# A two-layer diffusion trunk on one core: the row sum of the Fourier output weights made by an adding DMA, and an activation table loaded earlier

## The chip, the cores and the metric

The kernel runs on one core of a Trainium2 chip. The metric is device time in microseconds (us), from runs of the whole program; lower is better. Engines carry the profile's names: PE (TensorE matmul; PEld is its weight load), DVE (VectorE), ACT (ScalarE), POOL (GpSimd) and SP (SyncE, which here only issues DMAs). "Row" in the profile means one line of one of its views.

## The reference, cut to what matters

Everything is float32, with 512 latent tokens, 1024 channels, 256 context tokens and two layers. Layer 0 is attention, layer 1 is Fourier mixing with a linear map behind it; each ends with a gated convolutional feed-forward net. `rms_norm` stands before and behind every sub-layer, and each norm needs one reciprocal square root per token.

```python
def rms_norm(x, g):
    xf = x.astype(F32)
    y = xf * lax.rsqrt(jnp.mean(xf * xf, axis=-1, keepdims=True) + EPS)
    return (y * g.astype(F32)).astype(x.dtype)

def fourier_mix(h):
    b, l, d = h.shape
    hg = h.reshape(b, l, FNET_GROUPS, d // FNET_GROUPS).astype(F32)
    f = jnp.fft.fft2(hg, axes=(1, 3), norm="ortho").real
    return f.reshape(b, l, d).astype(h.dtype)

def conv_ffn(h, w_up, conv_w, conv_b, w_down):
    u = h @ w_up
    up = jnp.pad(u, ((0, 0), (1, 1), (0, 0)))
    u = up[:, :-2] * conv_w[0] + up[:, 1:-1] * conv_w[1] + up[:, 2:] * conv_w[2] + conv_b
    gate, val = jnp.split(u, 2, axis=-1)
    return (jax.nn.silu(gate) * val) @ w_down

# layer i:
h = modulate(rms_norm(x, norm_g[i, 0]), sh1, sc1)
y = attention_mixers(...) if i % 2 == 0 else fourier_mix(h) @ w_f
x = x + g1 * rms_norm(y, norm_g[i, 1])
h = modulate(rms_norm(x, norm_g[i, 2]), sh2, sc2)
x = x + g2 * rms_norm(conv_ffn(h, ...), norm_g[i, 3])
```

In the cosine and sine sums of the Fourier transform, channel c of a group of 256 and channel 256 - c share their values up to a sign. So `fourier_mix(h) @ w_f` needs, per group, only 128 rows of cosine sums times the sum of two rows of `w_f`, and 128 rows of sine sums times their difference. Making these sums and differences is what the main part of the change touches.

## The kernel before, in words

**Product.** A float32 product is made of three matmuls in a reduced-precision type. `split` rounds a tile to a high part (an ACT copy, `wh`, line 125) and takes the rest as a low part (a DVE subtraction, `wl`, the same line). `mm3` (lines 102 to 104) then issues high times high, high times low and low times high. In the profile, L102, L103 and L104 are these three. A weight tile can be used by L102 and L103 as soon as `wh` stands, and by L104 only when `wl` stands too.

**Order.** The program is written in one order, with priorities, and a scheduler places each engine's instructions in a queue of that engine's own; every queue runs in order. `fence` and `held` keep some instructions behind an earlier point of their engine. Tiles come from pools with a fixed number of places: `raw` (weights as loaded, by SP) has three, `wh` and `wl` have five each.

**Norms.** A column sum of squares is made by small matmuls (L184) into a `misc` tile. `rstd` (lines 187 to 195) makes the reciprocal root: an ACT table function gives `st_r` (L190), DVE scales the mean to `st_v` (L191), and a Newton step follows on DVE (L192 to L194). `spread` (L215) lays the result on a diagonal, a matmul (L218) carries it to all partitions, and ACT copies it out (L219). `rstd_all` (lines 201 to 210) does the same at the program's end on a wide tile. The ACT function needs a table of its own, and the feed-forward net's gate function (L1268) needs another; where the next function's table isn't there, the row `ACT_TABLE_LOAD` stands ahead of it.

**Feed-forward.** `ffn` has groups of up-projection, convolution, gate and down-projection. The last down phase of a layer (where `end` is true, line 1417) has no gate left in it. It runs over eight channel blocks d for the first half of the tokens, and then again for the second half; `mid`, between the two, starts the norm of the first half.

**Fourier output.** `w_f` is stored in eight tiles d, one per block of 128 output channels, each 128 partitions by 4 groups by 2 rows by 128 channels, 512 KB. Two tiles are loaded early into free places of `yT` (`fourier_load`, L1551); the other six go through `raw`. `fourier_weights(d)` makes the sum of the two rows (L1559: on DVE for d = 0, on POOL for the others) and their difference (L1560, DVE) in a third tile, and splits that. Each d then takes twelve matmuls with the difference (operand `B` in the profile), three with the Nyquist row (`N`) and twelve with the sum (`A`); DVE puts the two together (L1619, L1623).

**Beside it.** During this stage `up_weights_dma` fetches the first four up-projection weights of the layer behind it without using DVE. POOL issues a plain load into `xh` (L1118, 512 KB each). ACT writes the negative of its rounded value into `xl`, and POOL issues a second DMA of the same weights that adds into `xl` (L1122, the last one L1128). A DMA that adds is thus already in use four times. Its queue, the software queue of POOL, is apart from the hardware queue of SP. POOL also adds up squares (L277).

Of the kernel before, what the change touches and what calls it, by code (L numbers as in the profile page):

```python
# [10 lines left out]
F32 = mybir.dt.float32  # L11
# [68 lines left out]
def kernel(ctx: ExitStack, tc: tile.TileContext, a):  # L80
# [106 lines left out]
    def rstd(ps):  # L187
        w = ps.shape[1]
        v, t, r = (mk(cp, [P, W4], F32, "st_" + c, 2)[:, :w] for c in "vtr")
        S.activation(out=r, in_=ps, func=AF.Abs_reciprocal_sqrt, bias=eps, scale=1.0 / D)  # L190
        V.tensor_scalar(out=v, in0=ps, scalar1=1.0 / D, scalar2=EPS, op0=ALU.mult, op1=ALU.add)  # L191
        V.tensor_tensor(out=t, in0=r, in1=r, op=ALU.mult)  # L192
        V.scalar_tensor_tensor(out=t, in0=t, scalar=-0.5, in1=v, op0=ALU.mult, op1=ALU.mult)
        V.scalar_tensor_tensor(out=v, in0=t, scalar=1.5, in1=r, op0=ALU.add, op1=ALU.mult)  # L194
        return v
# [5 lines left out]
    def rstd_all(ps):  # L201
        ps = ps[:, :HT]
        r, t, v = (mk(cp, [P, HT], F32, "md_t", 4) for _ in range(3))
        R = mk(cp, [P, HT], F32, "Rs", 3)
        S.activation(out=r, in_=ps, func=AF.Abs_reciprocal_sqrt, bias=eps, scale=1.0 / D)
        S.activation(out=v, in_=ps, func=AF.Identity, bias=eps, scale=1.0 / D)
# [1025 lines left out]
    def ffn(l, xp, ready, pre, mid, gem, plain=None):  # L1232
# [146 lines left out]
        for gi, (f0, nch) in enumerate(GROUPS[l]):  # L1379
# [37 lines left out]
            if end:  # L1417
                pump(gem, 100)
                fence()
# [29 lines left out]
    with ExitStack() as es:  # L1449
# [98 lines left out]

        def fourier_load(d):
            r = yT[:, 3 * d + 1:3 * d + 3, :].rearrange("p a (g i c) -> p (a g) i c", i=2, c=P)  # L1550
# [3 lines left out]
        def fourier_weights(d, eng=G):  # L1554
            r = f_first[d] if d < 2 else raw([P, 4, 2, P], a["w_f"][d])

            pm = (yT[:, 6:8, :] if d in (3, 5) else yT[:, 2:4, :] if d == 1 else mk(cp, [P, 2, T], F32, "gacc")).rearrange(
                "p a (g c) -> p a g c", g=4)
            held(eng.tensor_tensor(out=pm[:, 0, :, :], in0=r[:, :, 0, :], in1=r[:, :, 1, :], op=ALU.add))  # L1559
            held(V.tensor_tensor(out=pm[:, 1, :, :], in0=r[:, :, 1, :], in1=r[:, :, 0, :], op=ALU.subtract))  # L1560
            wh, wl = wpair([P, 2, 4, P])
            split(wh, wl, pm)
# [24 lines left out]
        f_first = [fourier_load(d) for d in range(2)]  # L1587
# [7 lines left out]
        w_f = [fourier_weights(0, V)]  # L1595
# [8 lines left out]
        for d in range(KC):  # L1604
            wh, wl = w_f.pop() if w_f else fourier_weights(d)
            if d in (1, 3, 4, 5, 6):
# [78 lines left out]
def _layout(i):  # L1685
# [36 lines left out]
    w_f = np.stack([lo, hi], 1).reshape(4, 2, P, KC, P).transpose(3, 2, 0, 1, 4)  # L1722
# [22 lines left out]
```

## Time and profile before

| what | value |
|---|---|
| median of 3 runs (lowest to highest) | 1143.04 us (1142.85 to 1143.35) |
| the profiled execution: time, span | 1143.02 us, 1141.3 us |
| mean granted TensorE clock | 0.996 |
| busy PE, DVE, ACT, POOL in the span | 1113.0, 899.9, 595.6, 177.9 us |
| Fourier output stage: first and last matmul begin | 717.18, about 750.6 us |
| table load before `st_r` at the end of layer 0, of layer 1 | 664.51, 1112.78 us, 1.28 us each |

Times in the trace are counted from the start of the span. A timeline row gives start, duration, engine, line, operation, output and inputs; the bracket at its end is the engine's idle time before it, and which instruction ended it. A windows row gives, for one stretch, the length and then busy time and count for PE, PEld, DVE, ACT and POOL, the granted clock as a share of full speed, the share of the 16 DMA engines that was busy, and the GB/s.

### The profile page before, as it was taken

How to read it: one execution, taken by the hardware profiler on the slowest of the kernel's cores; microseconds unless marked ns; L12 is line 12 of the kernel's file. 1: busy time of each engine (PE TensorE's matmuls, PEld its weight loads, DVE VectorE, ACT ScalarE, POOL GpSimd, SP SyncE). 2: the span in 40 equal slices, each digit the busy share in tenths (PEclk: the TensorE clock that was granted, in tenths of full speed). 3: DMA queues.
4: the chain of work that ended last, by engine and by line, in shares of the span. 5: the costliest groups of instructions: out<-in, count | busy, mean ns of one | idle time of the engine just before them, and what ended most of it. 6: DMA issues, size and time to landing. Idle time of an engine off the chain costs nothing.

```text
span 1141.3 us, 19565 instructions
## 1 busy us (share of the span) xinstructions
PE 1113.0 (98%) x7810; PEld 965.9 (85%) x7810; DVE 899.9 (79%) x1469; ACT 595.6 (52%) x1068; POOL 177.9 (16%) x180
## 2 busy tenths in 40 slices
PE   9999999999999999999999999999999999999995
PEld 5689888868898978887898898779888898899995
DVE  4678777765679976987999668978998998879755
ACT  4342355665665633552465446557746555555533
POOL 1236422421420000000000143620000000000012
PEclk9999999999999999999999999999999999999998
DMA  9675101075143355535534401742215533323332
GB/s 367 258 240 212 38 1 38 27 264 190 38 186 111 109 196 213 222 120 203 195 108 174 131 5 59 233 119 109 74 47 165 185 103 116 103 91 94 103 143 74
DMA packets 33763, 155.83 MB, mean 137 GB/s; under 512 B 3460, under 2 KB 8196, under 8 KB 22024
## 3 DMA queue, kind: packets, MB, share of 16 engines
q1 hardware_dynamic: 32520, 150.39, 37.0%
q0 software_dynamic: 1152, 4.19, 1.6%
q8 instruction: 61, 1.00, 0.3%
q14 instruction: 30, 0.25, 0.1%
HBM read 148.28 MB, written 6.29 MB: 135 GB/s over the span
## 4 chain that ended last, share of the span: by engine, by line
PE 83%; DVE 10%; ACT 3%; issue 2%; DMA 1%; POOL 1%; DVEq 0%; POOLq 0%; ACTq 0%; SPq 0%
PE mm L102 24%; PE mm L103 22%; PE mm L104 22%; DVE wl L125 2%; PE PT L950 1%; DVE md_t L302 1%; PE O L102 1%; PE gm L527 1%; DMA raw<-in_w_up 1%; PE O L103 1%; PE gm L102 1%; PE gm L104 1%; PE gm L103 1%; PE O L104 1%; PE mm L178 1%
## 5 line engine op out<-in xcount | busy, mean ns | idle before, releaser
L125 ACT CAST wh<-raw 128x1024 fp32r<-128x1024 f32 (+2 forms) x207 | 190.6, 933 | 169.8 <-PE mm L103 118.7
L125 DVE TENSOR_TENSOR wl<-raw,wh 128x1024 fp32r<-128x1024 f32 (+2 forms) x197 | 214.8, 1098 | 54.3 <-ACT wh L125 54.0
L102 PE MATMUL mm<-hh,wh 128*128 128x256 f32 (+1 forms) x632 | 206.4, 327 | 1.5 <-ACT yT L925 0.9
L104 PE MATMUL mm<-hh,wl 128*128 128x256 f32 (+1 forms) x632 | 203.7, 323 | 0.0
L103 PE MATMUL mm<-hl,wh 128*128 128x256 f32 (+1 forms) x632 | 203.5, 322 | 0.0
L277 POOL TENSOR_TENSOR gacc<-gacc,sq 128x256 f32<-128x256 f32 (+1 forms) x33 | 27.9, 847 | 717.0 <-ACT sq L275 716.2
L102 PEld LDWEIGHTS mm<-hh,wh 128*128 128x128 f32 x632 | 118.9, 188 | 17.7 <-ACT sq L1194 4.4
L103 PEld LDWEIGHTS mm<-hl,wh 128*128 128x128 f32 x632 | 118.9, 188 | 11.1
L104 PEld LDWEIGHTS mm<-hh,wl 128*128 128x128 f32 x632 | 118.9, 188 | 10.5 <-DVE wl L125 0.4
L102 PE MATMUL mm<-zh,wh 128*128 128x256 f32 x384 | 109.1, 284 | 1.4 <-ACT sq L1197 0.8
L102 PE MATMUL mm<-xh,wh 128*128 128x512 f32 (+1 forms) x302 | 107.5, 356 | 0.0
L103 PE MATMUL mm<-xl,wh 128*128 128x512 f32 (+1 forms) x302 | 106.8, 354 | 0.0
L103 PE MATMUL mm<-zl,wh 128*128 128x256 f32 x384 | 106.6, 278 | 0.0
L104 PE MATMUL mm<-zh,wl 128*128 128x256 f32 x384 | 106.4, 277 | 0.0
L104 PE MATMUL mm<-xh,wl 128*128 128x512 f32 (+1 forms) x302 | 106.2, 352 | 0.0
L102 PEld LDWEIGHTS mm<-zh,wh 128*128 128x128 f32 x384 | 72.3, 188 | 5.7 <-ACT sq L1197 4.4
L103 PEld LDWEIGHTS mm<-zl,wh 128*128 128x128 f32 x384 | 72.2, 188 | 0.0
L104 PEld LDWEIGHTS mm<-zh,wl 128*128 128x128 f32 x384 | 72.1, 188 | 0.0
L102 PEld LDWEIGHTS mm<-xh,wh 128*128 128x128 f32 x302 | 56.8, 188 | 9.9 <-issue 1.6
L103 PEld LDWEIGHTS mm<-xl,wh 128*128 128x128 f32 x302 | 56.8, 188 | 8.6 <-issue 0.4
L104 PEld LDWEIGHTS mm<-xh,wl 128*128 128x128 f32 x302 | 56.7, 188 | 8.6
L1255 ACT ACTIVATE cv<-mm,cols 128x512 f32<-128x512 f32 x59 | 45.9, 777 | 28.6 <-PE mm L104 22.2
(435 smaller groups left out, 2802.3 us busy)
## 6 DMA issues: line engine op xcount, KB each, us to landing
raw<-in_w_up SPq DMA_DIRECT2D x42, 1024.0 KB, 4.9
xT<-in_mod_r SPq DMA_DIRECT2D x20, 1024.0 KB, 5.2
raw<-in_w_down SPq DMA_DIRECT2D x32, 384.0 KB, 3.1
raw<-in_mod_p SPq DMA_DIRECT2D x8, 1024.0 KB, 4.9
raw<-in_w_down SPq DMA_DIRECT2D x16, 512.0 KB, 4.1
raw<-in_w_in SPq DMA_DIRECT2D x6, 1024.0 KB, 7.8
yT<-in_mod_r SPq DMA_DIRECT2D x10, 512.0 KB, 6.5
raw<-in_w_out SPq DMA_DIRECT2D x4, 1024.0 KB, 5.0
```

The costliest lines, as they stand in the source:

```text
L102: i = PE.matmul(out, lhsT=ah, rhs=bh, start=start, stop=False, skip_group_check=skip)
L103: PE.matmul(out, lhsT=ah, rhs=bl, start=False, stop=False, skip_group_check=skip)
L104: return i, PE.matmul(out, lhsT=al, rhs=bh, start=False, stop=stop, skip_group_check=skip)
L125: i = S.copy(out=h, in_=src), eng.tensor_tensor(out=l, in0=src, in1=f(h), op=ALU.subtract)
L178: PE.matmul(ps[:32, :src.shape[1]], lhsT=ones32, rhs=src, start=True, stop=True)
L277: G.tensor_tensor(out=self.acc[:, sl], in0=self.acc[:, sl], in1=sq[:, sl], op=ALU.add)
L302: m = V.scalar_tensor_tensor(out=t, in0=yT[:, k, hs], scalar=der[:, l, gi, k:k + 1], in1=R, op0=ALU.mult, op1=ALU.mult)
L527: PE.matmul(ps[32 * q:32 * q + 32, :], lhsT=spad[:, k, :], rhs=w[:, q * T:(q + 1) * T], start=k == 0, stop=k == KC - 1)
L950: PE.transpose(out=pt[:, j * P:(j + 1) * P], in_=Ps[j][:, off:off + P], identity=ident)
L1255: S.activation(out=cv, in_=ps, func=AF.Identity, bias=bc, scale=wc[1])
```

## The change

It has four parts.

1. **rstd**: the DVE scaling of the mean stands ahead of the ACT function instead of behind it. Both read the same PSUM tile.
2. **rstd_all**: the same, and the scaling moves from ACT (an `Identity`, L206) to DVE.
3. **Table**: at the start of each layer's last down phase, ACT runs the reciprocal-root function once on a column of the last gated tile, with scale 0, into a scratch column. Its table is thus loaded there.
4. **Fourier weights**: `w_f` is stored with the two rows outermost (2 by 4 groups by 128). Three tiles instead of two are loaded early into `yT`. `fourier_pair(d)` makes the difference in place, over the second row (DVE), and then lets a DMA issued by POOL add the second row, read again from HBM (256 KB), to the first row in place. Pairs are written three tiles ahead of the weights that use them, and `split` takes the tile as it then stands. The POOL and DVE additions and the third tile are gone.

```diff
     def rstd(ps):
...
+        V.tensor_scalar(out=v, in0=ps, scalar1=1.0 / D, scalar2=EPS, op0=ALU.mult, op1=ALU.add)
         S.activation(out=r, in_=ps, func=AF.Abs_reciprocal_sqrt, bias=eps, scale=1.0 / D)
-        V.tensor_scalar(out=v, in0=ps, scalar1=1.0 / D, scalar2=EPS, op0=ALU.mult, op1=ALU.add)
...
     def rstd_all(ps):
...
+        V.tensor_scalar(out=v, in0=ps, scalar1=1.0 / D, scalar2=EPS, op0=ALU.mult, op1=ALU.add)
         S.activation(out=r, in_=ps, func=AF.Abs_reciprocal_sqrt, bias=eps, scale=1.0 / D)
-        S.activation(out=v, in_=ps, func=AF.Identity, bias=eps, scale=1.0 / D)
...
             if end:
+                S.activation(out=once, in_=g_[-1][0][:, 0:1].bitcast(F32), func=AF.Abs_reciprocal_sqrt, bias=eps, scale=0.0)
                 pump(gem, 100)
                 fence()
...
         def fourier_load(d):
-            r = yT[:, 3 * d + 1:3 * d + 3, :].rearrange("p a (g i c) -> p (a g) i c", i=2, c=P)
+            r = yT[:, 2 * d + 1:2 * d + 3, :].rearrange("p i (g c) -> p i g c", c=P)
             SY.dma_start(out=r, in_=a["w_f"][d])
             return r
-        def fourier_weights(d, eng=G):
-            r = f_first[d] if d < 2 else raw([P, 4, 2, P], a["w_f"][d])
-            pm = (yT[:, 6:8, :] if d in (3, 5) else yT[:, 2:4, :] if d == 1 else mk(cp, [P, 2, T], F32, "gacc")).rearrange(
-                "p a (g c) -> p a g c", g=4)
-            held(eng.tensor_tensor(out=pm[:, 0, :, :], in0=r[:, :, 0, :], in1=r[:, :, 1, :], op=ALU.add))
-            held(V.tensor_tensor(out=pm[:, 1, :, :], in0=r[:, :, 1, :], in1=r[:, :, 0, :], op=ALU.subtract))
+        pairs_f = {}
+        def fourier_pair(d):
+            r = pairs_f[d] = f_first[d] if d < 3 else raw([P, 2, 4, P], a["w_f"][d])
+            held(V.tensor_tensor(out=r[:, 1], in0=r[:, 1], in1=r[:, 0], op=ALU.subtract))
+            G.dma_start(out=r[:, 0], in_=a["w_f"][d][:, 1], accum_op=ALU.add)
+        def fourier_weights(d):
             wh, wl = wpair([P, 2, 4, P])
-            split(wh, wl, pm)
+            split(wh, wl, pairs_f[d])
             return wh, wl
...
-        f_first = [fourier_load(d) for d in range(2)]
+        f_first = [fourier_load(d) for d in range(3)]
...
-        w_f = [fourier_weights(0, V)]
+        fourier_pair(0)
+        fourier_pair(1)
+        w_f = [fourier_weights(0)]
+        fourier_pair(2)
...
             wh, wl = w_f.pop() if w_f else fourier_weights(d)
+            if d + 3 < KC:
+                fourier_pair(d + 3)
...
-    w_f = np.stack([lo, hi], 1).reshape(4, 2, P, KC, P).transpose(3, 2, 0, 1, 4)
+    w_f = np.stack([lo, hi], 1).reshape(4, 2, P, KC, P).transpose(3, 2, 1, 0, 4)
```

The change also moves instructions in the queues, since the scheduler places them anew. Three places matter.

POOL in the Fourier output stage, before. `gacc`, `yT` and `raw` hold weights of `w_f`; `xh` and `xl` are the up-projection weights; `acc` adds up squares. The words in brackets are what an instruction waits for (DMAHW and DMASW: a hardware or software DMA).

```order
L1559 TENSOR_TENSOR yT_68<-yT_68 128x512 [waits DMAHW5_49,DMAHW4_49,DVE_49]
L1559 TENSOR_TENSOR yT_68<-raw_7845 128x512 [waits DMAHW6_49]
L1118 DMA xh_7750<-in_w_up 128x1024 [waits PE_49,Activation_49]
L1118 DMA xh_7752<-in_w_up 128x1024 [waits PE_49]
L1118 DMA xh_7754<-in_w_up 128x1024
L1118 DMA xh_7756<-in_w_up 128x1024
L1559 TENSOR_TENSOR gacc_7801<-raw_7799 128x512 [waits DMAHW3_49,DVE_49]
L1559 TENSOR_TENSOR gacc_7893<-raw_7891 128x512 [waits DMAHW7_49,DVE_49]
L1122 DMA xl_7751<-in_w_up 128x1024 [waits Activation_49]
```

Two of the seven additions stand ahead of the `xh` loads here. POOL now, at the same place:

```order
L1562 DMA raw_7713<-in_w_f 128x512 [waits DMAHW3_49,DMAHW2_49,DVE_49]
L1118 DMA xh_7761<-in_w_up 128x1024 [waits PE_49,Activation_49]
L1562 DMA raw_7757<-in_w_f 128x512 [waits DMAHW7_49,DVE_49]
L1118 DMA xh_7763<-in_w_up 128x1024 [waits PE_49]
L1118 DMA xh_7765<-in_w_up 128x1024
L1118 DMA xh_7767<-in_w_up 128x1024 [waits DMASW0_49]
L1562 DMA raw_7814<-in_w_f 128x512 [waits DMASW1_49,DMAHW0_49,DVE_49,Activation_49]
L1122 DMA xl_7762<-in_w_up 128x1024 [waits DMASW2_49,Activation_49]
L1122 DMA xl_7764<-in_w_up 128x1024 [waits DMASW3_49,PE_49,Activation_49]
L277 TENSOR_TENSOR acc_7751<-acc_7751,sq_7807 128x512 [waits Activation_49]
L1562 DMA raw_7859<-in_w_f 128x512 [waits DMAHW1_49,DMASW4_49,DVE_49]
L1122 DMA xl_7766<-in_w_up 128x1024 [waits DMASW5_49,Activation_49]
```

The seven additions are gone from POOL. Ahead of these rows stand three adding DMAs (d = 0 to 2); those of d = 3 and 4 stand before and among the `xh` loads, that of d = 5 before the adding `xl` loads, that of d = 6 behind two of them, and that of d = 7 behind three.

DVE in the middle of the same stage, now. `wl_7811`, `wl_7856` and `wl_7902` are the low parts for d = 2, 3 and 4; L1628 and L1632 are the lines that were L1619 and L1623.

```order
L125 TENSOR_TENSOR wl_7811<-yT_68,wh_7810 128x1024 [waits DMASW2_49,Activation_49]
L1628 TENSOR_TENSOR yT_68<-mm_7730,qs_7746 128x256 [waits PE_49,Activation_49]
L1561 TENSOR_TENSOR raw_7814<-raw_7814 128x512 [waits DMAHW0_49]
L125 TENSOR_TENSOR wl_7856<-raw_7713,wh_7855 128x1024 [waits DMASW3_49]
L1632 TENSOR_TENSOR yT_68<-mm_7730,qs_7746 128x255 [waits Activation_49]
L125 TENSOR_TENSOR wl_7902<-raw_7757,wh_7901 128x1024 [waits DMASW5_49,DVE_49]
```

Every low part now waits for its adding DMA (DMASW), and behind it on DVE stands the work of an earlier d.

DVE at the norm of the first half at the end of layer 0, before:

```order
L191 TENSOR_SCALAR st_v_6973<-misc_6964 128x64 [waits Activation_49]
L192 TENSOR_TENSOR st_t_6974<-st_r_6975 128x64
L1281 TENSOR_TENSOR yT_68<-yT_68,mm_7046 128x256 [waits PE_49]
L193 SCALAR_TENSOR_TENSOR st_t_6974<-st_t_6974,st_v_6973 128x64 [waits DVE_49]
L194 SCALAR_TENSOR_TENSOR st_v_6973<-st_t_6974,st_r_6975 128x64 [waits DVE_49]
L215 TENSOR_TENSOR Rs_6981<-st_v_6973,con_66 128x256 [waits DVE_49]
```

Here an instruction that waits for PE stands inside the norm's chain. DVE now, at the same place:

```order
L190 TENSOR_SCALAR st_v_6974<-misc_6965 128x64 [waits PE_49]
L192 TENSOR_TENSOR st_t_6975<-st_r_6976 128x64 [waits Activation_49]
L193 SCALAR_TENSOR_TENSOR st_t_6975<-st_t_6975,st_v_6974 128x64 [waits DVE_49]
L194 SCALAR_TENSOR_TENSOR st_v_6974<-st_t_6975,st_r_6976 128x64 [waits DVE_49]
L215 TENSOR_TENSOR Rs_6982<-st_v_6974,con_66 128x256 [waits DVE_49]
L1281 TENSOR_TENSOR yT_68<-yT_68,mm_7047 128x256 [waits PE_49]
```

The scaling waits for PE instead of ACT (and ACT's function, now L191, waits for DVE), and the chain is no longer broken by L1281, which waits for a later matmul. On PE, L218 of this norm now stands behind 16 matmuls after the column sum instead of 29. On ACT, the table load has left its place just ahead of `st_r` and stands as L1419 behind the last gated tile, eighteen instructions ahead of `st_r`.

## The prediction

> **What bounds the kernel now.** I read the page's first lines and the chain of waits, then a table by stretch of the Fourier output stage, then the timelines of that stage and of the two norms that the change touches.
>
> ```profile
> span 1141.3 us, 19565 instructions
> PE 1113.0 (98%) x7810; PEld 965.9 (85%) x7810; DVE 899.9 (79%) x1469; ACT 595.6 (52%) x1068; POOL 177.9 (16%) x180
> PE 83%; DVE 10%; ACT 3%; issue 2%; DMA 1%; POOL 1%; DVEq 0%; POOLq 0%; ACTq 0%; SPq 0%
> ```
>
> PE is busy for 98% and holds 83% of the chain. A cut on DVE or POOL is worth something only where PE waits or its matmuls are spread. The stage that the main edit touches is such a place:
>
> ```profile
> 716.00:720.00 4.00, 3.19 (x22) 2.52 (x20) 4.00 (x7) 2.54 (x6) 4.00 (x4) 1.00 0.00 0
> 720.00:729.00 9.00, 8.58 (x58) 7.42 (x59) 6.93 (x13) 4.48 (x9) 4.50 (x5) 1.00 0.98 330
> 729.00:732.00 3.00, 3.00 (x28) 3.00 (x26) 3.00 (x2) 0.95 (x3) 3.00 (x4) 1.00 0.38 93
> 732.00:751.00 19.00, 17.64 (x138) 15.70 (x140) 14.77 (x19) 12.02 (x22) 12.51 (x10) 1.00 1.02 274
> 717.18 0.28 PE L102 MATMUL mm<-B,wh 128*128 128x256 f32 x1
> 744.98 0.38 PE L102 MATMUL mm<-N,wh 4*128 4x258 f32 x1
> 748.62 0.38 PE L102 MATMUL mm<-N,wh 4*128 4x258 f32 x1
> 750.36 0.29 PE L102 MATMUL mm<-A,wh 128*128 128x258 f32 x1
> 735.47 0.39 PE L104 MATMUL mm<-B,wl 128*128 128x256 f32 x1 [0.76 <-DVE wl L125]
> PE mm L104 <- DVE wl L125: 2.3, 4, 0.8
> ```
>
> From one Nyquist matmul to the next is one tile d: 748.62 - 744.98 = 3.64 us when nothing is late. Eight tiles want 29.1 us. The last tile's final group begins at 750.36, so after three matmuls 0.12 us apart the stage is through at about 750.75, 33.6 after 717.18. So 4.5 us are lost, 2.3 of them as waits for the DVE low part. And the DMA engines, idle from 716 to 720, are full (0.98, 1.02) for 28 of the next 31 us.
>
> **The change: removed work.** The third tile's arithmetic is what makes DVE late.
>
> ```profile
> 714.23 0.68 DVE L1560 TENSOR_TENSOR gacc<-yT 128x512 f32<-128x512 f32 x1
> 735.67 3.09 DVE L1560 TENSOR_TENSOR gacc<-raw 128x512 f32<-128x512 f32 x1
> 740.15 1.21 DVE L125 TENSOR_TENSOR wl<-gacc,wh 128x1024 fp32r<-128x1024 f32 x1
> 715.09 1.05 ACT L125 CAST wh<-gacc 128x1024 fp32r<-128x1024 f32 x1
> 735.50 1.47 POOL L1559 TENSOR_TENSOR gacc<-raw 128x512 f32<-128x512 f32 x1
> ```
>
> A difference takes 0.68 us alone and up to 3.09 while POOL adds beside it. Per tile DVE then needs 0.68 + 1.21 and two combinations, well under 3.64. If the sums are in time, DVE is out of the way and the eight tiles take 29.1 us.
>
> **What it adds in front.** The first tile used to be summed by DVE in 0.68 us. Now its sum is a DMA. The nearest rows are those that POOL already issues: first `xh` (512 KB, plain), then `xl` (512 KB, adding); the last two rows are the software queue over 716 to 729 us (only `xh`: packets, MB, share of 16 engines) and over 729.4 to 755 (only `xl`).
>
> ```profile
> 718.90 2.35 POOL L1118 DMA_DIRECT2D xh<-in_w_up  x4
> DMA to landing us min/median/max: 4.3/5.8/7.6
> 737.99 1.06 POOL L1122 DMA_DIRECT2D xl<-in_w_up  x1
> DMA to landing us min/median/max: 5.4/8.8/12.0
> q0 software_dynamic: 576, 2.10, 50.9%
> q0 software_dynamic: 576, 2.10, 43.7%
> ```
>
> The four plain transfers held 0.509 x 13 = 6.6 us of all engines, 1.65 each; the four adding ones 0.437 x 25.6 = 11.2, 2.8 each. A 256 KB sum is bounded by half of a plain one (0.8) and a whole adding one (2.8); I take half of an adding one, 1.4, the same kind by its bytes. The fastest plain landing, 4.3, less its 1.65 leaves 2.65 us of fixed latency; so a lone sum lands 2.65 + 1.4 = 4.0 us after its issue. The difference for d = 0 ends at about 714.4 (it takes the place of L1559), the sum lands at 718.5, ACT rounds it by 719.6 (1.05), DVE has the low part by 720.9 (1.21). PE's new order uses the high part in seven matmuls (0.9 us) before it needs the low one, so it starts at 719.7 instead of 717.18 and waits 0.3 more: 2.8 us later than now. Without another delay the stage is through at 719.7 + 0.3 + 29.1 = 749.1 instead of 750.75: **-1.7 us**. POOL itself gains time: an adding issue holds it for about 1.06 us, an addition for 1.47 at 735.50.
>
> [...]
>
> **What it adds behind.** The sums of d = 0 to 3 fall mostly into the idle 716 to 720. The later ones meet full engines. From 720 on, ahead of and with the sum of d = 6: four `xh` 6.6, about 1.6 left from the first four sums (5.6 less 4.0), sums of d = 4 and 5 2.8, `raw` of d = 6 1.6 (as a plain 512 KB), two `xl` 5.6, itself 1.4: 19.6 us, so 739.6, and landed a good us later, or earlier by what SP's queue leaves behind it. Then 1.05 + 1.21 + hand-overs = 2.35: low part at 742 to 743. PE wants it at 719.7 + 0.3 + 6 x 3.64 + 0.4 = 742.2. For d = 7 come one more `xl` 2.8, `raw` of d = 7 1.6 and itself 1.4, and part of a 1 MB `raw` load that is queued by SP: landing 743.5 to 747, low part 746 to 749.5; wanted at 745.9. So the stage's end is late by 0 to 4 us; I take 2.5. **Fourier stage: -1.7 + 2.5 = +0.8 us** (bounds: -1.7 if no sum is late; with 2.8 a sum, 1.4 x 8 = 11 more engine time, of which the idle stretches hide about 3: +9).
>
> Who waits behind a late sum: on DVE the combinations of d = 4, and so the PSUM places of d = 7, which needs the same sum anyway; on SP the 1 MB `raw` loads, whose casts come only at 765; the last `xl`, issued behind the sum of d = 7 and used from 757.4, landed in all likelihood by 755.
>
> ```profile
> 757.41 0.50 PE L102 MATMUL mm<-hh,xh 128*128 128x258 f32 x2
> 765.20 1.98 ACT L125 CAST wh<-raw 128x1024 fp32r<-128x1024 f32 x2
> ```
>
> **Table and scaling.** The norm at the end of layer 0, from its column sum on, and an ACT row from the start of the same down phase:
>
> ```profile
> 664.71 0.32 PE L184 MATMUL misc<-sq,ones 128*32 128x64 f32 x8
> 664.51 1.28 ACT L190 ACT_TABLE_LOAD   x1
> 665.80 0.32 ACT L190 ACTIVATE st_r<-misc,eps 128x64 f32<-128x64 f32 x1
> 666.29 0.22 DVE L192 TENSOR_TENSOR st_t<-st_r 128x64 f32<-128x64 f32 x1
> 667.54 0.22 DVE L193 SCALAR_TENSOR_TENSOR st_t<-st_t,st_v 128x64 f32<-128x64 f32 x1
> 668.05 1.38 DVE L215 TENSOR_TENSOR Rs<-st_v,con 128x256 f32<-128x256 f32 x1
> 668.25 0.28 PE L104 MATMUL mm<-xh,wl 128*128 128x256 f32 x1
> 669.58 0.67 PE L218 MATMUL misc<-Rs,con 128*128 128x256 f32 x2 [1.05 <-DVE Rs L215]
> 644.46 1.05 ACT L125 CAST zh<-raw 128x1024 fp32r<-128x1024 f32 x1 [2.22 <-DMA raw<-in_w_down]
> ```
>
> The load holds `st_r` back by some 0.7 us, and L1281 holds L193 back by a further 1.0. Without both, scaling starts at 665.1, the function at 665.35, L192 at 665.7, L215 at 666.5 to 666.9. PE's L218 is reached 13 matmuls earlier, at 668.4 - 13 x 0.115 = 666.9. **About -0.95** of the 1.05; nothing is gained where POOL's table work still slows L215 to 1.38. The load's new place costs nothing: ACT is idle there for 2.22 us ahead of the cast at 644.46, and the down phase's first products read weights that are cast before. At the end of layer 1 the wait is only 0.36, and the end hangs on later rows:
>
> ```profile
> 1116.93 0.70 PE L218 MATMUL misc<-Rs,con 128*128 128x256 f32 x2 [0.36 <-DVE Rs L215]
> 1131.27 0.42 DVE L207 TENSOR_TENSOR md_t<-md_t 128x256 f32<-128x256 f32 x1 [2.23 <-ACT md_t L206]
> ```
>
> There the wide scaling moves from ACT behind the function to DVE ahead of it: one 0.4 us step for another, **0**; the earlier L218 may give up to -0.3.
>
> The swap by itself costs: each engine waits for the other, so scaling (0.22) comes before the function instead of beside L192's wait: about +0.1 on each of 16 chains, hidden by matmuls in most. At 753 two norms follow each other:
>
> ```profile
> 753.43 0.32 ACT L190 ACTIVATE st_r<-misc,eps 128x64 f32<-128x64 f32 x1 [0.44 <-PE misc L184]
> 753.63 0.43 DVE L215 TENSOR_TENSOR Rs<-st_v,con 128x256 f32<-128x256 f32 x1
> 754.20 0.67 PE L218 MATMUL misc<-Rs,con 128*128 128x256 f32 x2
> ```
>
> In DVE's new queue the second scaling, whose sum stands only at 753.4, comes before the first norm's L193. So L215 moves from 753.63 to about 754.15: **+0.5**. Elsewhere **+0.1**, bounds 0 and 1.6.
>
> **Sum.** 0.8 - 0.95 + 0.5 + 0.1 = +0.45 on the profiled 1143.02 us (span 1141.3 and 1.7 around it; the median is 1143.04): **1143.5 us**. What a measurement of this kernel can tell from no change is 0.2%, 2.3 us.
>
> **Rivals.**
> *No sum is late.* DMA shares need not add up as I did; if SP's loads yield, the stage ends at -1.7: 1143.02 - 1.7 - 0.35 = 1141.0. For it: 1.9 idle us at 729 to 732. Against: 1.02 from 732.
> *A sum is nearly only latency.* At the plain price of 0.8 it lands 3.4 us after issue, PE starts 0.6 earlier, and eight sums hold 6.4 us of engines instead of 11.2, so none is late: 1140.4. [...] Against: `xl` held 1.7 times the engine time of `xh`.
> *The sums of d = 6 and 7 queue behind the adding `xl` loads.* The software queue is served in order: the sum of d = 7 has three `xl` ahead of it, which took 5.4 to 12.0 us to land. If it is issued at 740 and takes 9 to 12, it lands at 749 to 752, low part by 751.5 to 754.5, 5.5 to 8.5 late: -1.7 + 7 - 0.35 = +5, 1148. It decides from a landing after 746.5 on. Against: it is half as long as an `xl`, and POOL is freed of its additions and issues sooner.
> *The table or the swap does not help.* If L215 still runs beside POOL, or the function's wait on DVE eats it, -0.95 falls to 0: 1144.4.
>
> **Numbers.** Forecast 0.40 (of it 0.33 within 0.2%, 0.03 faster, 0.04 slower); no sum late 0.22 (0.11 faster, 0.11 same); only latency 0.10, faster; queued behind `xl` 0.23, slower; table no help 0.05, same. Faster 0.24, same 0.49, slower 0.27. The forecast's own range is 1141.5 to 1145.7. The range 1139.5 to 1148.5 takes in both cheap cases and over half of the dear one.
>
> **What would show it.** Right: L1559 gone; first Fourier matmul near 719.7 less what the layer before gains; differences near 0.68; PE waits for `wh` or `wl` at d = 6 and 7 released late by DMASW; no table load at 664, L218 without a 1 us wait; L215 near 754.1 less shifts. Wrong: sums that land 3 us or 9 us after issue, waits in the middle of the stage, or a changed time outside these places, where the scheduler also moved instructions of layer 0's feed-forward net.

## The result, and the profile after

| | before | after |
|---|---|---|
| median of 6 runs (lowest to highest) | 1143.36 us (1142.85 to 1145.16) | 1150.78 us (1150.1 to 1151.89) |
| the profiled execution: time, span | 1143.02, 1141.3 us | 1150.4, 1148.6 us |
| mean granted clock | 0.996 | 0.990 |

The ratio is 1.006, with a 95% interval of 1.005 to 1.007: **slower by 0.6%**, some 7 us. The prediction was 1143.5 us, "same" the likeliest, and its range ended at 1148.5. It was wrong.

The page's first lines and its chain of waits, after:

```profile
span 1148.6 us, 19590 instructions
PE 1118.2 (97%) x7810; PEld 971.3 (85%) x7810; DVE 895.3 (78%) x1469; ACT 595.8 (52%) x1069; POOL 170.9 (15%) x181
PE 84%; DVE 7%; DMA 4%; ACT 3%; issue 2%; POOL 0%; DVEq 0%; ACTq 0%; POOLq 0%; SPq 0%
```

On the chain DVE fell from 10% to 7% and DMA rose from 1% to 4%. PE is busy for 5 us longer with as many instructions, so its matmuls ran slower somewhere. The table by stretch of the Fourier output stage says where (the columns are those of the prediction's table: busy time and count for PE, PEld, DVE, ACT and POOL, granted clock, DMA share, GB/s):

```profile
716.00:720.00 4.00, 1.78 (x15) 1.50 (x13) 2.62 (x8) 1.73 (x4) 2.67 (x5) 1.00 0.83 138
720.00:729.00 9.00, 8.89 (x43) 8.17 (x44) 6.73 (x9) 6.68 (x11) 3.63 (x7) 0.62 1.08 271
729.00:732.00 3.00, 3.00 (x25) 2.87 (x25) 2.02 (x5) 1.67 (x3) 2.25 (x3) 1.00 0.93 281
732.00:751.00 19.00, 16.81 (x112) 15.17 (x111) 6.02 (x10) 7.78 (x14) 7.75 (x7) 0.91 1.02 251
720.25:727.00 6.75, 6.75 (x29) 6.30 (x30) 4.57 (x6) 4.79 (x7) 2.95 (x5) 0.50 1.06 235
747.25:754.25 7.00, 6.42 (x27) 5.97 (x28) 3.18 (x6) 3.17 (x8) 3.02 (x3) 0.52 0.92 218
```

DVE did as foreseen: from 732 to 751 it is busy for 6.02 us, where it was 14.77. But the granted clock, 1.00 all through this stage in the profile of before, fell to half for 6.75 us and again for 7 us (the last two rows). Each fall follows a wait on PE. The timeline of PE has all its waits of this stage, and its last matmul there:

```profile
720.11 0.50 PE L102 MATMUL mm<-B,wh 128*128 128x256 f32 x1 [2.33 <-ACT wh L125]
746.57 0.39 PE L102 MATMUL mm<-B,wh 128*128 128x256 f32 x1 [1.43 <-ACT wh L125]
747.83 0.58 PE L104 MATMUL mm<-B,wl 128*128 128x256 f32 x1 [0.76 <-DVE wl L125]
757.64 0.28 PE L104 MATMUL mm<-A,wl 128*128 128x258 f32 x1
```

The stage lasts from 720.11 to 757.64, 37.5 us; before it lasted 33.4 (717.18 to 750.61). Why `wh` of d = 6 stands only at 746.5 is told by the chain of waits inside the stage (start, us, what; in its last two rows are the cast and the subtraction of d = 6):

```profile
721.52 6.03 DMA raw<-in_w_f
...
729.12 7.16 DMA raw<-in_w_f
...
737.49 7.96 DMA raw<-in_w_f
745.48 1.05 ACT wh L125
746.55 1.24 DVE wl L125
```

These are three DMAs one behind the other: the adding DMA of d = 4, the load of `raw` for d = 6 by SP, and the adding DMA of d = 6. The load waits until a place of `raw` is free. Before, a place was free as soon as the sum and the difference had read it, and the last three loads went out from 722.58 us on (that of d = 6 at 723.70). Now the split is its last reader, so the place of d = 3 is free only when `wl` of d = 3 is made; d = 6 is loaded at 729.12 and its sum is issued at 737.49:

```profile
727.82 1.22 DVE L125 TENSOR_TENSOR wl<-raw,wh 128x1024 fp32r<-128x1024 f32 x1
729.12 1.79 SPq L134 DMA_DIRECT2D raw<-in_w_f  x2
736.37 0.69 DVE L1561 TENSOR_TENSOR raw<-raw 128x512 f32<-128x512 f32 x1 [3.42 <-DMA raw<-in_w_f]
737.49 0.87 POOL L1562 DMA_DIRECT2D raw<-in_w_f  x1 [2.51 <-DVE yT L1628]
742.89 0.88 POOL L1562 DMA_DIRECT2D raw<-in_w_f  x1 [0.28 <-issue]
745.48 1.04 ACT L125 CAST wh<-raw 128x1024 fp32r<-128x1024 f32 x1 [3.87 <-DMA raw<-in_w_f]
750.19 1.04 ACT L125 CAST wh<-raw 128x1024 fp32r<-128x1024 f32 x1 [1.92 <-DMA raw<-in_w_f]
751.27 1.23 DVE L125 TENSOR_TENSOR wl<-raw,wh 128x1024 fp32r<-128x1024 f32 x1 [3.16 <-ACT wh L125]
```

From the issue of the load to the end of the low part (746.55 + 1.23 = 747.8) it takes d = 6 18.7 us. The pairs are written three tiles ahead, which is 3 x 3.64 = 10.9 us of PE's time.

### The profile page after: what moved, and what is told of

Its sections match the earlier page's. It is cut to its first block, busy times and chain, and to the rows that moved or that the text cites. A ratio compares the mean times of both kernels' runs of the same rounds, so it can differ in the third digit from the quotient of the medians.

```text
span 1148.6 us, 19590 instructions
## 1 busy us (share of the span) xinstructions
PE 1118.2 (97%) x7810; PEld 971.3 (85%) x7810; DVE 895.3 (78%) x1469; ACT 595.8 (52%) x1069; POOL 170.9 (15%) x181
## 4 chain that ended last, share of the span: by engine, by line
PE 84%; DVE 7%; DMA 4%; ACT 3%; issue 2%; POOL 0%; DVEq 0%; ACTq 0%; POOLq 0%; SPq 0%
PE mm L102 24%; PE mm L104 23%; PE mm L103 23%; DMA raw<-in_w_f 2%; DVE wl L125 1%; PE PT L950 1%; PE O L102 1%; PE gm L527 1%; DMA raw<-in_w_up 1%; PE gm L102 1%; PE O L103 1%; PE gm L104 1%; PE gm L103 1%; PE O L104 1%; PE mm L178 1%
## 5 line engine op out<-in xcount | busy, mean ns | idle before, releaser
L125 ACT CAST wh<-raw 128x1024 fp32r<-128x1024 f32 (+2 forms) x212 | 195.8, 936 | 177.2 <-PE mm L103 118.6
L125 DVE TENSOR_TENSOR wl<-raw,wh 128x1024 fp32r<-128x1024 f32 (+2 forms) x202 | 220.7, 1101 | 62.1 <-ACT wh L125 61.8
L277 POOL TENSOR_TENSOR gacc<-gacc,sq 128x256 f32<-128x256 f32 (+1 forms) x33 | 28.7, 870 | 717.0 <-ACT sq L275 716.2
```

Source lines behind the costliest of these rows:

```text
L125: i = S.copy(out=h, in_=src), eng.tensor_tensor(out=l, in0=src, in1=f(h), op=ALU.subtract)
L277: G.tensor_tensor(out=self.acc[:, sl], in0=self.acc[:, sl], in1=sq[:, sl], op=ALU.add)
```

## The experiments

Times are medians, with the number of runs; a ratio is to the kernel before, run beside it on the same chip, with its 95% interval (it need not be the quotient of two medians). The last three columns are from one profiled execution each: begin of the first and the last matmul of the Fourier output stage, and its length.

| kernel | median us (runs) | ratio | first | last | length |
|---|---|---|---|---|---|
| before | 1143.36 (6) | 1 | 717.18 | 750.61 | 33.4 |
| after | 1150.78 (6) | 1.006 [1.005, 1.007] | 720.11 | 757.64 | 37.5 |
| only_fourier | 1149.97 (5) | 1.0046 [1.0031, 1.0062] | 721.41 | 759.58 | 38.2 |
| no_fourier | 1145.13 (10) | 1.0008 [0.9997, 1.0018] | 718.90 | 753.81 | 34.9 |
| swap_only | 1145.58 (10) | 1.0016 [1.0007, 1.0026] | 720.38 | 755.27 | 34.9 |
| table_only | 1142.72 (10) | 0.9989 [0.9980, 0.9998] | 717.22 | 752.16 | 34.9 |
| table_fourier | 1148.68 (4) | 1.0044 [1.0029, 1.0059] | 719.74 | 758.81 | 39.1 |
| fill_first | 1151.99 (4) | 1.0070 [1.0048, 1.0091] | 721.63 | 757.87 | 36.2 |
| fill_both | 1157.62 (4) | 1.0107 [1.0086, 1.0129] | 721.70 | 762.57 | 40.9 |
| probe4 | 1147.18 (8) | 1.0028 [1.0018, 1.0038] | 722.95 | 756.05 | 33.1 |
| no_xl | 1147.09 (8) | 1.0031 [1.0014, 1.0048] | 721.86 | 753.03 | 31.2 |
| dve_late | 1146.44 (9) | 1.0028 [1.0013, 1.0044] | 721.33 | 754.47 | 33.1 |
| dve_first_late | 1146.13 (10) | 1.0013 [1.0002, 1.0024] | 718.86 | 753.24 | 34.4 |
| dve_all | 1146.75 (10) | 1.0024 [1.0015, 1.0034] | 718.63 | 753.12 | 34.5 |
| nf_fill | 1147.22 (8) | 1.0025 [1.0011, 1.0038] | 718.60 | 754.94 | 36.3 |
| best_fill | 1145.90 (11) | 1.0013 [1.0005, 1.0022] | 718.50 | 752.37 | 33.9 |
| table_dve | 1143.19 (10) | 1.0002 [0.9989, 1.0016] | 717.17 | 752.02 | 34.9 |
| table_v | **1139.16 (4)** | **0.9958 [0.9941, 0.9974]** | 717.21 | 747.42 | 30.2 |

Many of these kernels spread over several us from run to run (no_xl from 1144.24 to 1151.21). So a difference of less than some 1.5 us between two rows proves little by itself.

### Which part costs what

**only_fourier** is part 4 alone: the changed kernel with `rstd`, `rstd_all` and the table as before.

```diff
-        V.tensor_scalar(out=v, in0=ps, scalar1=1.0 / D, scalar2=EPS, op0=ALU.mult, op1=ALU.add)
         S.activation(out=r, in_=ps, func=AF.Abs_reciprocal_sqrt, bias=eps, scale=1.0 / D)
+        V.tensor_scalar(out=v, in0=ps, scalar1=1.0 / D, scalar2=EPS, op0=ALU.mult, op1=ALU.add)
...
-                S.activation(out=once, in_=g_[-1][0][:, 0:1].bitcast(F32), func=AF.Abs_reciprocal_sqrt, bias=eps, scale=0.0)
```

> Part 4 alone (Fourier weights by adding DMAs), parts 1 to 3 undone. The changed kernel was 7.4 us slower than before, and its trace gains 1.4 us at the end of layer 0. Both theories put the loss into the Fourier stage: 1151 to 1152.5 us, 8 to 9 us over before.

**no_fourier** is the other half, parts 1 to 3: the changed kernel with `fourier_load` and `fourier_weights` as before.

```diff
-        def fourier_pair(d):
...
+        def fourier_weights(d, eng=G):
...
+            held(eng.tensor_tensor(out=pm[:, 0, :, :], in0=r[:, :, 0, :], in1=r[:, :, 1, :], op=ALU.add))
```

> Parts 1 to 3 alone, part 4 undone. Both theories: 0.5 to 1.5 us faster than before, 1141.8 to 1142.8; granted clock 1.0 all through the Fourier stage.

Part 4 alone costs 0.46%, 5.3 us. That is the larger piece, though less than was expected. Parts 1 to 3 were expected to gain 0.5 to 1.5 us, with the clock at 1.0 all through the stage. They gained nothing (1.0008), and the granted clock was 0.57 over the 4.00 us from 722.5 to 726.5. Comparing the begin of the same instructions with before, no_fourier's DVE is 1.7 us ahead at 697 and its PE 0.9, but at 712 both are 1.7 behind. So something between the layers takes away what the norm gave.

**table_only** (part 3 put into the kernel before) and **swap_only** (parts 1 and 2, all else as before) split that half.

```diff
@@ table_only: the kernel before with
             if end:
+                S.activation(out=once, in_=g_[-1][0][:, 0:1].bitcast(F32), func=AF.Abs_reciprocal_sqrt, bias=eps, scale=0.0)
@@ swap_only: the changed kernel without that line, and with fourier_weights as before
```

> Part 3 alone (the earlier table load), with the function ahead of the scaling as before. If the table load is what gained time at the end of layer 0: PE is 1.0 to 1.6 us ahead of before at 690 us, as with parts 1 to 3. If the order of scaling and function did it: less than 0.5 us ahead.

> Parts 1 and 2 alone (scaling ahead of the function), table load and Fourier weights as before. Parts 1 to 3 came out 0.9 us over before and part 3 alone 1.3 under it. If the swap is what takes the gain back: 1.5 to 2.5 us over before, with PE's 0.7 us wait for hl at 701 and 0.96 for the column matmul at 708 in its trace. If it is their working together: within 0.5 of before.

The table gains 0.11%, 1.3 us, and the swap costs 0.16%, 1.8 us. The trace of table_only, compared with before by the begin of the same instructions, shows where the gain lies. It is 1.13 us behind up to 660 and 0.06 behind from 690 to 720: the end of layer 0 gains 1.1 us. From 721 to 726 it loses 1.5 in a fall of the clock (0.57 from 721.5 to 725.5, last section). At the end of layer 1, where L218 no longer waits, it goes from 1.18 behind to 0.41 behind, a gain of 0.8.

PE's waits between the layers, in swap_only (`Z` is the result of the transform over the channels, `hl`, made by L360, the low part of its input):

```profile
702.61 0.39 PE L104 MATMUL misc<-wh,hl 128*128 128x256 f32 x1 [0.69 <-DVE hl L360]
706.14 0.39 PE L102 MATMUL misc<-wh,hh 128*128 128x256 f32 x1 [0.78 <-DVE Z L125]
709.25 0.83 PE L378 MATMUL misc<-ones,yT 128*128 128x2 f32 x6 [0.94 <-ACT yT L364]
```

and the row of its table by stretch behind them:

```profile
710.50:714.00 3.50, 3.47 (x17) 3.17 (x16) 1.96 (x6) 2.20 (x6) 0.00 (x0) 0.51 0.00 0
```

Before has 0.65 and 0.47 for `Z` there, and neither of the other two waits. With the swap the scheduler places DVE's work of this stretch in another order: between the last L1485 and the first subtraction of `Z` (L125) stand four instructions of L360 instead of two. The waits at 702.61 and 709.25 come with that order, and the granted clock falls to 0.51 for 3.5 us behind them. no_fourier, which has the swap too, shows the same waits (0.69, 0.78 and 0.96) and the same fall (0.51 from 709 to 712.5). The traced execution of swap_only took 1148.24 us, well over its median, so sizes read from it do not add up to the 1.8 us; but the swap's cost is, as far as the traces show, mostly not in the norms that it edits. No run puts the old order back with the swap in place.

**table_fourier** is parts 3 and 4 without the swap.

```diff
@@ the changed kernel, with rstd and rstd_all as before
```

> Parts 3 and 4 without the swap. If the parts add up (all four +6.9, swap +2.2): 4 to 5.5 us over before. If the loss of the Fourier part hangs on PE's being early, because the sums come at a fixed time whatever PE does: 6 to 7.5 over.

It measured 1.0044, 5.0 us over before, as it should if the parts add up, though not clearly below part 4 alone. Added up: 5.3 for the Fourier weights, 1.8 for the swap, -1.3 for the table make 5.8, against 6.9 for all. The interval of each is 1 us or more on either side, so the 1.1 left needs no cause of its own, and none was found.

### Is it the late first sum and the clock behind it?

The front loses 2.33 us to the first sum and then half the clock. **fill_first** puts ten matmuls, whose result nobody reads, ahead of the first Fourier matmul, so that the wait leaves PE no longer idle.

```diff
+            cold = fill({0: 10}[d]) if d in {0: 10} else None
             for g in range(4):
-                mm3(pq[:, :256], wh[:, 1, g, :], wl[:, 1, g, :], B[0][:, g, :], B[1][:, g, :], g == 0, g == 3)
+                m3 = mm3(pq[:, :256], wh[:, 1, g, :], wl[:, 1, g, :], B[0][:, g, :], B[1][:, g, :], g == 0, g == 3)
```

> The changed kernel with ten idle-time matmuls (32 x 256, some 0.24 us each, their result unused) on PE between the last matmul ahead of the Fourier output stage and its first. Clock theory (PE idle for 2.3 us lets the granted clock fall to 0.5 for 6.8 us, which costs 3.4): the clock stays at 1.0 from 720 to 728, 3.3 us less, 1147.5. Transfer theory (the sums are late and the queues are full, the clock is by the way): no gain, 1150.8 or a little more.

The clock did what the edit wanted, and the time did not follow. Two rows of its table by stretch, and PE's only wait in the stage:

```profile
720.25:727.00 6.75, 6.75 (x47) 5.50 (x46) 5.76 (x8) 3.92 (x5) 2.93 (x5) 1.00 1.05 239
744.50:751.50 7.00, 4.93 (x22) 4.70 (x23) 3.78 (x6) 4.54 (x9) 2.14 (x2) 0.51 0.90 219
```

```profile
746.57 0.58 PE L102 MATMUL mm<-N,wh 4*128 4x258 f32 x1 [5.05 <-ACT qs L1640]
```

At full clock (1.00 instead of 0.50 in the same 6.75 us) PE is ahead until the middle of d = 5, and waits there for 5.05 us. The copy on ACT that it waits for stands in ACT's queue behind the cast of d = 6, and the sum of d = 6 lands only at 744.1. It was issued 2.7 us earlier than in after (734.83), but landed only 1.3 us earlier. So the slow stretch at 720 was hidden behind the late sum. It is not what costs the time; this theory fell.

**fill_both** also filled the waits ahead of d = 6 and d = 7 (nine and five matmuls).

```diff
+            cold = fill({0: 10, 6: 9, 7: 5}[d]) if d in {0: 10, 6: 9, 7: 5} else None
```

> As the run before, and nine such matmuls ahead of tile 6 and five ahead of tile 7. Clock theory: granted clock 1.0 all through the stage, 1144 to 1146. Transfer theory: 1150.8 or more.

It came out at 1.0107. The added matmuls changed the order of other work too: the sum of d = 7 landed at 753 instead of 750.2. It settles nothing on the second fall of the clock.

**probe4** takes the kernel before and makes it wait in the same place, by four copies of the first `wh` onto itself on ACT.

```diff
         w_f = [fourier_weights(0, V)]
+        for _ in range(4):
+            held(S.copy(out=w_f[0][0], in_=w_f[0][0].bitcast(F32)))
```

> The kernel before with four copies of the first Fourier tile's high part onto itself on ACT (1.05 us each), which hold that tile back without any DMA. Clock theory: PE idles for about 3 us at 718, the granted clock falls to 0.5 for 6.8 us, 6 to 8 us over before. Without a fall: 2.5 to 4.5 us over before.

PE waits for 5.46 us and then has half the clock for some 10 us (a row of the timeline, and one of the table by stretch):

```profile
722.95 0.58 PE L102 MATMUL mm<-B,wh 128*128 128x256 f32 x1 [5.46 <-ACT wh L1597]
```

```profile
722.00:732.50 10.50, 9.55 (x41) 8.88 (x42) 6.68 (x10) 5.96 (x9) 5.81 (x4) 0.51 1.05 318
```

That is some 10 us at half speed, but the stage is no longer than before (33.1 against 33.4 us). It ends 5.4 us later, about what it began later (5.8), and the kernel is 1.0028, 3.2 us, slower. Before, the stage loses 4.5 us as it is, much of it to a DVE that is late; while PE is slow, DVE catches up, and the first wait is PE's only one. So here the late start cost at most its own length, and the half clock behind it nothing that shows.

### Is it the sums of d = 6 and 7 behind the loads that add?

This is the rival at 1148. In the trace of after the software queue landed its transfers in the order of their issue: the sum of d = 5 landed at 736.5, two `xl` (issued at 729.17 and 730.76) at 740.1 and 742.6, the sum of d = 6 at 745.45, an `xl` at 748.9, the sum of d = 7 at 750.2. **no_xl** leaves out the four adding `xl` loads.

```diff
             if i:
-                G.dma_start(out=ws[i - 1][0][1], in_=ws[i - 1][1], accum_op=ALU.add)
+                pass
...
-        G.dma_start(out=wl, in_=src, accum_op=ALU.add)
```

> The changed kernel without the four adding DMAs into xl (their 2 MB; xl then holds only the negative of xh, so the up-projection of four weights comes out without its low part; nothing else is left out). Queue theory (the sums of tiles 6 and 7 queue behind xl on full DMA engines and set the stage's end, the lower clock at its start is hidden behind them): both sums land within 5 us of their issue instead of 8, PE's wait at tile 6 is gone or under 0.5 us, 4 to 5 us less: 1146 to 1147. Clock theory alone: the wait at the first tile and its 6.8 us at half clock stay, at most 2 us less.

**dve_late** keeps them, and makes the sums of d = 6 and 7 on DVE, in place (the first row times two plus the difference).

```diff
-            G.dma_start(out=r[:, 0], in_=a["w_f"][d][:, 1], accum_op=ALU.add)
+            if d in (6, 7):
+                held(V.scalar_tensor_tensor(out=r[:, 0], in0=r[:, 0], scalar=2.0, in1=r[:, 1], op0=ALU.mult, op1=ALU.add))
+            else:
+                G.dma_start(out=r[:, 0], in_=a["w_f"][d][:, 1], accum_op=ALU.add)
```

> The changed kernel, but the sums of tiles 6 and 7 made by DVE in place (twice the first row plus the difference, 0.7 us each) instead of by DMA. Queue theory: no wait at tile 6, no second stretch at half clock; the first wait and its half clock are now bare, 3.5 to 5 us less: 1146 to 1147.5. Clock theory alone: 1.7 to 3.4 less.

Both take off about half of the loss, 3.3 and 3.7 us (1.0031 and 1.0028 instead of 1.006). ACT's cast for d = 6, in no_xl and then in dve_late, stands at 741.6 and 739.3 instead of 745.5:

```profile
741.61 1.05 ACT L125 CAST wh<-raw 128x1024 fp32r<-128x1024 f32 x1 [0.68 <-DMA raw<-in_w_f]
```

```profile
739.32 1.06 ACT L125 CAST wh<-raw 128x1024 fp32r<-128x1024 f32 x1
```

In no_xl the sum of d = 6 is issued no earlier than in after (737.79 against 737.49), but lands 3.79 us later instead of 7.96. PE does not wait at d = 6 (only for 0.33 us at d = 7, whose sum took 5.97 us instead of the 5 expected), the clock falls no second time in the stage (1.00 from 729 to 757), and the stage takes 31.2 us. So of the three DMAs in a row, the one that decides is the last, held up behind `xl`; the late load of the place sets its issue, but without `xl` that would have done. The run does not tell the wait in the queue from the engine time that `xl` takes, since both go with it. And `xl` is not the only load that holds up a sum: that of d = 5 took 7.9 us in after and 8.5 in no_xl, behind the `xh` loads. PE did not wait for it.

In dve_late PE does not wait at d = 6 either, but at d = 5, 2.27 us at 743.81, which was not expected. The sum of d = 5, a DMA there, was cast only at 737.10, and on DVE its low part stands behind the difference of d = 7, which waited 2.51 us for its load by SP. The clock did not fall after this wait (1.00 from 732 to 757).

### What is left: the first sum, and the freed DVE

**dve_first_late** also makes the first sum on DVE; **dve_all** all eight, so that part 4 adds no DMA.

```diff
-            if d in (6, 7):
+            if d in (0, 6, 7):
```

> As the run before, and the sum of tile 0 made by DVE too. Both theories: no wait of over 1 us in the stage and clock 1.0 through it; 4 to 5.5 us less again: 1141.5 to 1143, at or below before. The difference to the run before is the bare price of the first wait (2.3 us) with its half clock (3.4).

> The changed kernel with all eight sums made by DVE in place; no added DMA. Two passes of 0.7, one of 1.2 and two of 0.4 are 3.4 us a tile on DVE against 3.64 on PE: if POOL's squares do not slow them, 1141 to 1142.5; if DVE falls behind as before, 1143 to 1144.

Without the wait for the first sum the kernel is at 1.0013, by the ratios 1.7 us better than dve_late. The two intervals overlap and the medians differ by 0.3 us, so a price of the first sum is not shown. What is left is near what parts 1 to 3 cost by themselves (1.0008). Both kernels were expected near or below before and are not. In dve_first_late PE waits three times behind 719 (0.41, 0.21 and, for `N` from ACT, 0.93 us), and the clock falls (0.54 from 722 to 729.5). The longest of these waits comes from a sum that is still a DMA, that of d = 1. ACT's queue has the cast of d = 1 ahead of that of `N`, and the cast waits 1.50 us for the sum:

```profile
721.15 1.05 ACT L125 CAST wh<-yT 128x1024 fp32r<-128x1024 f32 x1 [1.50 <-DMA yT<-in_w_f]
722.10 0.36 ACT L125 CAST N<-mm 4x258 fp32r<-4x258 f32 x1
```

So not all of its sums were in time. In dve_all no sum is a DMA; PE waits there for DVE, 1.72 us at 720.63 and 1.40 at 744.61. On DVE the sums and differences of d = 0 to 2 and the low part of d = 0 stand ahead of the low part of `B` (719.90).

**nf_fill** and **best_fill** ask whether the clock's fall at 709 makes the difference: four matmuls that nobody reads ahead of those of L378, in no_fourier and in dve_first_late.

```diff
+                    if h == 1 and i == n == 0:
+                        w = mk(pps, [P, T], F32, "mm", 6)
+                        for _ in range(4):
+                            k = PE.matmul(w[:32, :256], lhsT=ones32, rhs=xT[:, 0, :256], start=True, stop=True)
```

> Parts 1 to 3 alone (part 4 undone), with four idle-time matmuls on PE (32 x 256, unused) between the first and the second column matmul of line 378, where PE waited 0.96 us and the granted clock then fell to 0.5 from 709. If the gain of parts 1 to 3 is eaten by that fall: clock 1.0 from 705 to 715, 1.5 to 2 us less than without them, 1143 to 1143.7, and less spread. If it is eaten by waits alone: no change, 1145.

> The version with the sums of tiles 0, 6 and 7 on DVE, and the four idle-time matmuls at line 378. Clock theory for the rest: no fall at 709, 1.7 us less than without them (1146.1), 1143.5 to 1144.5; below 1142 only if the fall at 722 goes too.

The fall at 709 is gone in both (1.00 from 709 to 712.5), and neither gained. In nf_fill PE then waits for `B`, which DVE makes, and the clock falls there (0.51 from 721 to 731.5):

```profile
721.36 0.58 PE L103 MATMUL mm<-B,wh 128*128 128x256 f32 x1 [2.48 <-DVE B L125]
```

In best_fill PE waits 2.18 us for `N`, again behind the sum of d = 1 on ACT. What is filled at one place comes back as a wait at the next, and each edit that moved a fall of the clock moved the waits too. Two traces price a fall all the same: table_only has PE's waits of this stage as before has them, within 0.2 us each, and one fall of some 3.4 us (0.57 over 4.00 us, last section), and its stage takes 34.9 us instead of 33.4. no_fourier and swap_only, with the same weights code and one such fall (0.57 over 4.00 us in each), take 34.9 too. So by these traces a fall that no other delay hides costs some 1.5 us, a little under half of its length.

### A version that beats both

**table_dve** has part 3, and part 4 with the sums of d = 0, 6 and 7 on DVE; there is no swap. **table_v** has part 3 and none of part 4: the weights as before, with the third tile, but every sum on DVE instead of POOL.

```diff
@@ the kernel before, with the line of table_only and
-        def fourier_weights(d, eng=G):
+        def fourier_weights(d, eng=V):
```

> As the run before, with the sums of tiles 0, 6 and 7 on DVE. If these three sums are the loss of part 4: 0 to 1.5 us under before, at most 1 us off part 3 alone. If sums by DMA cost in the middle of the stage as well: 1 or more over before.

> Part 3 alone, and the sums of the Fourier weights as before but all on DVE instead of POOL (no DMA). If POOL's additions only slowed DVE (differences of up to 3.09 us beside them): 1 to 3 us under part 3 alone, 2 to 4 under before. If DVE has no room for the sums: above part 3 alone.

table_dve is not told from before (1.0002, and 1143.19 against 1143.81 us beside it): part 4 gains nothing there either. PE waits 1.08 us for `N`, again behind the sum of d = 1, and 1.46 for a low part at 745. table_v takes 1139.16 us, 0.9958 of before, 4.8 us less, and beats the changed kernel by more than 11. Its stage takes 30.2 us, close to the 29.1 of eight tiles without a wait. Two rows of its table by stretch, and four of the timeline: DVE's sum and difference in the middle of the stage, a difference beside POOL, and PE's last matmul:

```profile
720.00:729.00 9.00, 9.00 (x71) 8.45 (x70) 8.22 (x13) 5.61 (x11) 1.20 (x2) 1.00 0.92 313
732.00:751.00 19.00, 18.35 (x169) 15.29 (x168) 14.04 (x26) 10.62 (x23) 8.95 (x7) 1.00 0.94 275
```

```profile
727.17 0.68 DVE L1562 TENSOR_TENSOR gacc<-raw 128x512 f32<-128x512 f32 x1
727.77 0.68 DVE L1563 TENSOR_TENSOR gacc<-raw 128x512 f32<-128x512 f32 x1
736.26 1.76 DVE L1563 TENSOR_TENSOR gacc<-raw 128x512 f32<-128x512 f32 x1
747.42 0.28 PE L104 MATMUL mm<-A,wl 128*128 128x258 f32 x1
```

DVE does seven more additions and is no busier: 25.8 us over the stage, against 27.5 before. Before, four of the differences took 1.34 to 3.09 us beside POOL's additions; here sums and differences take 0.67 or 0.68, but for three of 1.20 to 1.89, each while POOL adds up squares (L277). The clock stays at 1.00. Against table_only this one edit is worth 0.31%, 3.5 us; of the 4.7 us between their stages, 1.5 are the fall of the clock in table_only. The edit does two things at once, which no run tells apart: POOL's additions of weights no longer slow DVE, and a sum takes 0.68 us on DVE instead of 1.28 to 2.44 on POOL.

## Why the prediction was wrong, point by point

**What bounds the stage before: right.** DVE was late, and POOL's additions made its instructions long (differences of up to 3.09 us). The differences came out at 0.67 to 0.69 us once POOL's additions were gone, and table_v's 30.2 us show that the lost 4.5 us could nearly all be had.

**The first sum: right.** It was to land 4.0 us after issue and landed after 3.88 (issued at 715.11). The first Fourier matmul was put at 719.7, and came at 720.11 in a profile that was 0.46 late at 712. The fall of the clock behind the wait was not foreseen.

**The engine time of a sum: right.** 1.4 us was taken. The rows of the software queue from 690 to 760, before and then after (packets, MB, share of 16 engines):

```profile
q0 software_dynamic: 1152, 4.19, 25.4%
```

```profile
q0 software_dynamic: 2304, 6.29, 43.2%
```

(0.432 - 0.254) x 70 / 8 = 1.56 us each.

**The sums of d = 6 and 7: here the forecast failed.** The step was the sum of engine times, "19.6 us: so 739.6", and a good us until landed. The sum of d = 6 landed at 745.45, its low part stood at 747.8 (742 to 743 predicted, 742.2 wanted); that of d = 7 landed at 750.2, low part 752.5 (746 to 749.5 predicted, 745.9 wanted). They were 5.6 and 6.6 us late, not 0 to 4. Adding up engine time fails in two ways here. It lets a transfer begin at any time, while this sum could not be issued before 737.49. And it leaves out what the other queue takes meanwhile: from 729 to 751 the two queues shared the engines like this (the 1 MB load of SP at 738.85 was not in the sum for d = 6). With the same issue time but no `xl`, no_xl had the sum at 741.6 and was 3.3 us faster than after; with these two sums on DVE, dve_late was 3.7 faster.

```profile
q0 software_dynamic: 1014, 2.88, 64.2%
q1 hardware_dynamic: 506, 2.70, 35.6%
```

The third rival had it: sums in order behind the adding `xl`, 5.5 to 8.5 us late, 1148. It was given 0.23 because the sums are short; behind two `xl` the short sum of d = 6 took 7.96 us to land, and 3.79 in no_xl. Its -1.7 was still too kind, it counted no fall of the clock, and it had the swap at only +0.6.

**The gain of the freed DVE, -1.7: not found.** With the sums of d = 0, 6 and 7 on DVE (dve_first_late, 1.0013) the kernel is no faster than without part 4 (no_fourier, 1.0008). The gain asked for all sums in time, and no version with sums by DMA had that: where the first sum is on DVE, the sum of d = 1 holds up ACT and with it `N`. In table_v ACT casts `N` (717.89) ahead of d = 1 (718.52), no sum is a DMA, and the waits are absent. So -1.7 stands untested for timely sums by DMA.

**The table: right at layer 0, too small at layer 1.** -0.95 at the end of layer 0 and 0 to -0.3 at the end of layer 1 were predicted. table_only's trace gained 1.1 and 0.8, and the kernel 1.3 us. PE's wait at the end of layer 1 had shown only 0.36; what else the earlier L218 released was not traced.

**The swap: mis-sized.** +0.5 at 753 is what no_fourier shows (+0.45 from 749 to 758). But the term of +0.1 elsewhere, with bounds of 0 and 1.6, was some 1.3 us (1.8 in all, 0.8 to 3.0 by the interval), and by the traces it came from another order of DVE's work around 700. The prediction named such moves only as something that would make it wrong; the order of the instructions had to be read there too.

## What to carry to other kernels

An addition may be handed to an adding DMA only if the lead covers the whole chain of a buffer (place free, load, difference, sum, split: 18.7 us here, against a lead of three tiles, 10.9 us of PE's time), with the sum at the end of what its queue already holds (behind two `xl` that of d = 6 took 7.96 us to land); adding up the engine time of transfers does not show this. A late sum also holds up what stands behind its reader in the same queue, as `N` behind the cast of d = 1 (PE waits 0.93 us for it in dve_first_late). Where one engine's work slows another's, try first to give that work to the slowed engine: in table_v DVE did POOL's seven additions itself and was busy for less time. A small edit in a scheduled program is to be judged by every queue that it reorders.

## What the runs showed of the hardware

The granted clock fell to half behind short waits of PE. In after, 2.33 us of idleness at 717.8 were followed by 0.50 for 6.75 us. In swap_only three waits of 0.69, 0.78 and 0.94 us within 8 us were followed by 0.51 for 3.5. Taken as time at 0.50, the low stretches come to 3.4 us in swap_only and table_only (0.51 over 3.50 us, 0.57 over 4.00), 6.75 and 6.7 in after (0.50 over 6.75, 0.52 over 7.00) and 10.3 in probe4 (0.51 over 10.50). Equal waits did not always end in a fall: before and table_only both wait for 0.30 and 0.61 us around 718 and 720, at the same times within 0.05 us, and only table_only fell afterwards (the second wait in before, the same in table_only, and the row by stretch of table_only):

```profile
720.10 0.39 PE L104 MATMUL mm<-B,wl 128*128 128x256 f32 x1 [0.61 <-DVE wl L125]
```

```profile
720.15 0.39 PE L104 MATMUL mm<-B,wl 128*128 128x256 f32 x1 [0.61 <-DVE wl L125]
```

```profile
721.50:725.50 4.00, 4.00 (x23) 4.00 (x22) 2.67 (x4) 0.47 (x2) 2.21 (x1) 0.57 1.07 322
```

What sets the two apart no run here shows.

Half the clock cost less than its length. In table_only a fall of some 3.4 us with no other change cost 1.5 us. In probe4 a wait of 5.46 us and some 10 us at half clock cost 3.2 us in all, because the stage had waits of its own that went away. And the transfers on POOL's queue landed in the order of their issue (after), and a 256 KB sum took 3.79 us with none ahead of it (no_xl) and 7.96 us behind two 512 KB ones (after).
